# A hybrid decoder step: unbudgeted last top-ks, early key transpositions in the score products' PSUM tiles, and PLE weight splits on ScalarE and VectorE

## The chip, the cores and the metric

The kernel runs on one core of a Trainium2 chip. The metric is the device time of one execution in microseconds; the median of three runs before the change is 1889.77 us (1889.49 to 1900.7). The profile shows one further execution of the same program, with every engine's instructions: TensorE (PE), VectorE (DVE), ScalarE (ACT), GpSimd (POOL), and the queue of the sync engine (SP), which issues nearly all transfers.

## The reference

One layer over a prompt of 2048 rows and 64 sample rows. Cut to what bears on the change:

```python
z = rmsnorm(x, norm_g) @ w_in              # split into q, k, v, qi, ki, wi, ga, u, vm, gm
score = sum_h wi[h] * relu(qi[h] @ ki.T)   # indexer scores
idx = top_k(where(causal, score, -inf), 256)     # keys of each query row
o = softmax(q @ k[idx].T / 8) @ v[idx]           # per block of 128 rows
mix = concat(o * silu(ga), gelu(u) * s * silu(gm))
r = x + mix @ w_out
y = r + sigmoid(rmsnorm(r, ple_norm_g) @ w_ple_gate) * (p @ w_ple_proj)
```

Everything is fp32. A product is made from two fp32r parts of each factor, a high part and the remainder (hi and lo), in three matmuls: hi·hi, hi·lo and lo·hi.

## The kernel before

The prompt is cut into 16 blocks of 128 rows, and the sample rows are block 16, written SB in the code. There are three phases.

**Phase A** computes the input projection in rounds, and between its steps `pump` gives out pieces of the indexer: score products (PE writes them into the PSUM tiles `dots`, of which there are two), and top-ks (a search on ACT and DVE for the threshold of each row, ending in a mask that is written to `s_mask`). `pump` takes a budget of work and counts each piece against it. At the end of phase A stands the part of the output projection that needs no attention: for each block, `gm_load` reads the gated rows from `s_gm`, `gm_split` (L567) transposes them on PE into a PSUM tile `tp` (two buffers) from which ACT makes `hhi` (L124) and DVE the remainder (L125), and `gm_product` makes one output half as 12 matmuls into `z` (L579, L580, L583). I call these 12 matmuls a unit. ACT copies `z` out as `hlo` (L585) and SP writes it to `s_r` (L588). There are 34 units, two of them (block 16) with 8 matmuls.

The counter `u` numbers the units. From `u > EARLY` on, each unit lets the generator `early` go one step. At `u == DRAIN`, `pump(1e9)` gives out all that is left of the indexer and `early` becomes `prep_early`, which prepares the attention: it transposes the query blocks (L1036, two groups of four) and the 16 key tiles (L1021, four transposes each) into PSUM tiles that its argument supplies. For a key tile i, SP loads `b_kr` and `b_vr` (L991, L992; two buffers each), ACT doubles the keys into `b_kd` (L1015; two buffers), PE transposes, ACT writes `Kst` (L1023), DVE subtracts the remainder in it (L1024), and POOL makes the value parts `Vst` (L1026, L1027). At `u == FLAG_AT` a matmul of one column (L897) sums a flag of all top-ks, DVE writes it as `f_fl` (L899), and each engine reads it (L902) ahead of a branch that decides on a repeat of the search for rows where the threshold failed.

**Phase B** is the attention per block, scores `b_s` first (L1103, L1104). **Phase C** does the rest of the output projection (from `w_out`), the norm, and the last two products with `w_ple_gate` and `w_ple_proj`. These weights come as 8 and 2 tiles of 128 rows: `raw_load` (L1415) puts one into `c_raw` (three buffers) and `raw_split` makes `c_h` (L1421 on ACT, L1423 on another engine) and `c_l` (L1424). The residual row block is `c_x` (L1437, POOL), the norm's statistics are `c_st` (L1495, L1496, POOL), and the normed rows `c_rn` (L1497, DVE).

The program is not run in the order of the code: a scheduler orders each engine's queue at build time, and every engine then works its queue in order. An engine waits at an instruction until its operands are ready and the tile it writes is free.

Of the kernel before, what the change touches and what calls it, by code (L numbers as in the profile page):

```python
# [9 lines left out]
F32 = mybir.dt.float32  # L10
# [101 lines left out]
class Builder:  # L112
# [85 lines left out]
    def phase_a(self, eb):  # L198
        tc, nc, I, O = self.tc, self.nc, self.I, self.O
        with ExitStack() as es:  # L200
# [95 lines left out]
            def load_out(j):  # L296
                wh, wl = (t.rearrange("p k n -> p (k n)")[:, :2048].rearrange("p (k n) -> p k n", k=4) for t in halves(328))
                for i in range(8):
                    raw = rp.tile([128, 328], F32, name="raw")[:, :256]
                    k, c0 = i // 2, i % 2 * 256  # L300
                    nc.sync.dma_start(raw, I["w_out"][0, 512 + k * 128:640 + k * 128, j * 512 + c0:j * 512 + c0 + 256])
                    nc.gpsimd.tensor_scalar(wh[:, k, c0:c0 + 256], raw, 1.0, 1.0, op0=OP.mult, op1=OP.mult)
                    nc.gpsimd.tensor_tensor(wl[:, k, c0:c0 + 256], raw, wh[:, k, c0:c0 + 256].bitcast(F32), OP.subtract)
                return wh, wl
# [141 lines left out]
            blocks_due, dots, tops = [], [], []  # L446

            primed, active, steps = [], [None], [0]

            credit, turn = [0.0], [0]  # L450

            def pump(budget):
                credit[0] = min(credit[0], 0.0) + budget
                while credit[0] > 0 and (blocks_due or primed or dots or tops):
                    if not primed and blocks_due and not (dots and (active[0] == SB or steps[0] < 4)):
                        b = blocks_due.pop(0)
                        primed.append((b, self.sample_idx() if b == SB else self.idx(b)))
                        next(primed[0][1])
                    if not dots and primed and len(tops) < 2:
                        active[0], g = primed.pop()  # L460
                        steps[0] = 0
                        dots.append(g)
                    turn[0] ^= 1
                    l = (dots, tops)[turn[0]]
                    if l:
                        try:
                            v = next(l[0])
                            steps[0] += l is dots
                            if isinstance(v, tuple):
                                tops.append(self.topk(*v))  # L470
                                v = 0
                            credit[0] -= v
                            if l is tops and not (dots or primed or blocks_due):
                                tops.append(tops.pop(0))
                        except StopIteration:
                            l.pop(0)
# [15 lines left out]
            for si, (r, c) in enumerate(seq):  # L492
                blocks = ROUNDS[r]
                name = CH[c][0]
# [63 lines left out]
            def gm_load(b):  # L558
                gm[b] = hp.tile([128, 8, 128], F32R, name="hlo").rearrange("p a b -> p (a b)").bitcast(F32)[:self.rows(b)]
                nc.sync.dma_start(gm[b][:, :512], self.s_gm[b][:self.rows(b)])  # L560

            def gm_split(b):
                P = self.rows(b)
                hh = gmT[b] = hp.tile([128, 8, 128], F32R, name="hhi")
                ps = self.tp.tile([128, 4, 128], F32, name="tp")
                for k in range(4):
                    nc.tensor.transpose(ps[:, k, :P], gm[b][:, k * 128:k * 128 + 128], ident[:P, :P])  # L567
                if b == SB:
                    self.split(hh[:, 0:4, 0:64], hh[:, 0:4, 64:128], ps[:, :, 0:64])
                else:  # L570
                    self.split(hh[:, 0:4], hh[:, 4:8], ps)

            def gm_product(b, j, w):
                P = self.rows(b)
                hh = gmT[b]
                wh, wl = w
                zt = self.zp.tile([128, 512], F32, name="z")
                for k in range(4):
                    nc.tensor.matmul(zt, lhsT=hh[:, k], rhs=wh[:, k], start=(k == 0), stop=False)  # L579
                    nc.tensor.matmul(zt, lhsT=hh[:, k], rhs=wl[:, k], start=False, stop=(b == SB and k == 3))  # L580
                if b != SB:
                    for k in range(4):
                        nc.tensor.matmul(zt, lhsT=hh[:, 4 + k], rhs=wh[:, k], start=False, stop=(k == 3))  # L583
                y = gm[b][:, (1 - j) * 512:(1 - j) * 512 + 512]
                nc.scalar.activation(y, zt[:P], AF.Copy)  # L585
                if b == SB:
                    nc.vector.tensor_tensor(y, zt[64:128], y, OP.add)
                nc.sync.dma_start(self.s_r[b][:P, j * 512:j * 512 + 512], y)  # L588

            order = list(range(NB)) + [SB]  # L590
            early, u = iter(()), 0
            for n in range(0, 17, 2):
                if n == 0:
                    for b in order[:2]:
                        gm_load(b)
                    for b in order[:2]:
                        gm_split(b)
                for j in range(2):
                    for b in order[n:n + 2]:
                        gm_product(b, j, ws[j])  # L600
                        if n == 0 and j == 0 and b == 0:
                            ws.append(load_out(1))
                        if j == 1 and b + 2 < 17:
                            gm_load(b + 2)
                        pump(self.idx_rate)
                        u += 1
                        if u > EARLY:
                            next(early, None)
                        if u == DRAIN:
                            pump(1e9)  # L610
                            ei.close()
                            early = self.prep_early(eb, lambda: self.tp.tile([128, 4, 128], F32, name="tp"))
                        if u == FLAG_AT:
                            self.flag(self.tp.tile([128, 4, 128], F32, name="tp")[:, 0])
                for b in order[n + 2:n + 4]:
                    gm_split(b)
# [774 lines left out]
    def phase_c(self):  # L1391
        tc, nc, I, O = self.tc, self.nc, self.I, self.O
        V = nc.vector
        ident = self.ident
        with ExitStack() as es:
# [10 lines left out]
            tp = pool("c_tp", 2, space=PSUM)  # L1406
# [10 lines left out]
            def raw_split(name, k, eh, el):  # L1417
                hi, lo = W[name][k]
                raw = raw_tiles.pop((name, k))
                if eh is nc.scalar:  # L1420
                    nc.scalar.activation(hi, raw, AF.Copy)  # L1421
                else:
                    eh.tensor_scalar(hi, raw, 1.0, 1.0, op0=OP.mult, op1=OP.mult)  # L1423
                el.tensor_tensor(lo, raw, hi.bitcast(F32), OP.subtract)  # L1424
# [4 lines left out]
            def load(b):  # L1429
                P = self.rows(b)  # L1430
                mix = pre.tile([128, 512], F32, name="c_mix", bufs=2)[:P]
                r = pre.tile([128, D], F32, name="c_r")[:P]
                x = xp.tile([128, D], F32, name="c_x")[:P]
                nc.sync.dma_start(mix, self.s_o[b][:P])
                nc.sync.dma_start(r, self.s_r[b][:P])
                nc.sync.dma_start(x, I["x_sample"].rearrange("a t d -> (a t) d") if b == SB else I["x_prompt"][0, b * 128:b * 128 + 128])
                nc.gpsimd.tensor_tensor(x, x, r, OP.add)  # L1437
                st[b] = (mix, x)
# [45 lines left out]
            def stage1a(b):  # L1484
                mid[b] = transposed(b, st[b][0], 4, "o")
# [51 lines left out]
            gates = [("w_ple_gate", k) for k in range(8)] + [("w_ple_proj", k) for k in range(2)]  # L1537
# [3 lines left out]
            for n in range(LEAD + 1):  # L1541
                load(blocks[n + 1])
                stage1b(blocks[n])
                stage1a(blocks[n + 1])
                for q in range(n * per, min(n * per + per, len(gates))):
                    raw_split(*gates[q], nc.gpsimd if q % 3 == 2 else nc.scalar, nc.gpsimd if q % 3 == 1 else V)
                    if q + 3 < len(gates):
                        raw_load(*gates[q + 3])
            for n in range(2):
# [37 lines left out]
```

## Time and profile before

| | |
|---|---|
| Median of three runs | 1889.77 us |
| Profiled execution | 1893.5 us, of which the span is 1891.7 us |
| PE busy | 1833.5 us (97%) |
| DVE, ACT, POOL busy | 66%, 54%, 33% |
| Mean granted PE clock | 0.988 of full speed |

The span runs from the first to the last instruction of the profiled execution. Rows of the timeline give start, duration, engine, line, and the tile written with those read; in brackets stands the engine's idle time just before the row and what released it. A repeated matmul is one row with its count. A matmul's shown duration includes its pipeline; the spacing of starts tells its cost.

### The profile page before, as it was taken

The page shows a single profiled execution, that of the slowest core. Times are in us where ns is not written, and L with a number is a line of the kernel's source. Part 1 is how long each engine was busy: PE and PEld are TensorE (multiplying, and loading weights), DVE is VectorE, ACT ScalarE, POOL GpSimd, SP SyncE. Part 2 cuts the span into 40 slices and gives each one's busy share as a digit, 9 for nine tenths or more (in the row PEclk, how much of TensorE's full clock was granted, in tenths as well). Part 3 has the DMA queues.
Part 4 walks back from the last instruction along what each step waited for, and adds up shares of the span by engine and source line. Part 5 has one row for each costly group of instructions (what it writes and reads, how often), then busy time and mean ns, then how long its engine had stood idle before and what let it go on. Part 6 is the DMA issues. An engine that isn't in the chain of part 4 may idle for free.

```text
span 1891.7 us, 33962 instructions
## 1 busy us (share of the span) xinstructions
PE 1833.5 (97%) x11974; PEld 1601.0 (85%) x11974; DVE 1242.1 (66%) x3631; ACT 1018.2 (54%) x1909; POOL 623.5 (33%) x950
## 2 busy tenths in 40 slices
PE   7989998999999999999988899999999999999998
PEld 7989988999999999999877678778777777888887
DVE  5597665378878547788752789888999764233321
ACT  4244335256565636766654888868788653122121
POOL 5482562342012324013303442233221364222221
PEclk9989999999999999999999899999999999999999
DMA  8855756645344554554553442233220373223211
GB/s 253 247 163 179 223 189 203 215 131 161 119 162 146 194 174 145 163 170 134 176 188 128 134 112 76 64 108 94 61 78 12 100 258 122 74 95 104 94 37 45
DMA packets 243806, 261.53 MB, mean 138 GB/s; under 512 B 83176, under 2 KB 209840, under 8 KB 243248
## 3 DMA queue, kind: packets, MB, share of 16 engines
q1 hardware_dynamic: 237744, 240.45, 40.5%
q0 software_dynamic: 5888, 18.88, 3.4%
q8 instruction: 95, 1.56, 0.3%
q14 instruction: 79, 0.65, 0.1%
HBM read 171.90 MB, written 87.37 MB: 137 GB/s over the span
## 4 chain that ended last, share of the span: by engine, by line
PE 83%; DVE 5%; DMA 5%; POOL 2%; issue 2%; ACT 2%; SPq 0%; DVEq 0%; POOLq 0%; ACTq 0%
PE z L319 10%; PE z L320 10%; PE z L322 10%; PE b_o L1155 7%; PE b_tp L1138 6%; PE c_mm L1471 5%; PE c_mm L1470 5%; PE c_mm L1474 5%; PE b_s L1103 3%; PE dots L688 3%; PE dots L689 3%; PE b_s L1104 3%; PE z L579 1%; PE z L580 1%; PE z L583 1%
## 5 line engine op out<-in xcount | busy, mean ns | idle before, releaser
L319 PE MATMUL z<-whi,hhi 128*128 128x256 f32 (+1 forms) x1792 | 463.0, 292 | 10.5 <-ACT vt L414 5.0
L320 PE MATMUL z<-wlo,hhi 128*128 128x256 f32 (+1 forms) x1792 | 454.1, 287 | 0.2 <-DVE wlo L289 0.2
L319 PEld LDWEIGHTS z<-whi,hhi 128*128 128x128 f32 x1792 | 341.9, 191 | 21.2 <-issue 8.5
L320 PEld LDWEIGHTS z<-wlo,hhi 128*128 128x128 f32 x1792 | 341.8, 191 | 6.1 <-DVE wlo L289 1.5
L322 PE MATMUL z<-whi,hlo 128*128 128x256 f32 (+1 forms) x1792 | 262.6, 286 | 0.0
L322 PEld LDWEIGHTS z<-whi,hlo 128*128 128x128 f32 x1792 | 237.7, 190 | 2.0
L693 DVE SCALAR_TENSOR_TENSOR big<-dots,sgn,big 128x1024 f32<-128x1024 f32 (+7 forms) x176 | 179.2, 1018 | 52.3 <-ACT dots L691 50.6
L125 DVE TENSOR_TENSOR b_pt<-b_tp,b_pt 128x512 fp32r<-128x512 f32 (+1 forms) x288 | 183.4, 655 | 12.1 <-ACT b_pt L124 11.0
L691 ACT ACTIVATE dots<-dots 128x1024 f32<-128x1024 f32 (+7 forms) x176 | 140.3, 801 | 87.7 <-PE dots L689 82.9
L1155 PE MATMUL b_o<-b_pt,Vst 128*128 128x512 f32 x544 | 184.1, 424 | 1.2 <-DVE b_pt L125 0.8
L124 ACT ACTIVATE b_pt<-b_tp 128x512 fp32r<-128x512 f32 (+1 forms) x288 | 155.5, 578 | 48.2 <-PE b_tp L1138 45.4
L1138 PE MATMUL b_tp<-mats,b_sm 128*128 128x128 f32 x1088 | 172.0, 275 | 2.3 <-DVE b_pt L125 1.8
L1112 ACT ACTIVATE b_sm<-b_sm,b_st 128x128 f32<-128x128 f32 (+15 forms) x128 | 154.7, 1210 | 16.2 <-DVE b_st L1105 15.4
L829 ACT ACTIVATE bfw<-big,tk 128x384 bf16<-128x384 f32 (+14 forms) x105 | 136.4, 1300 | 45.7 <-DVE tk L849 27.9
L1138 PEld LDWEIGHTS b_tp<-mats,b_sm 128*128 128x128 f32 x1088 | 131.5, 141 | 34.1 <-ACT b_sm L1112 4.8
L1103 PE MATMUL b_s<-Kst,b_qh 128*128 128x512 f32 (+3 forms) x320 | 139.5, 439 | 4.1 <-DVE b_st L1105 2.2
L1105 DVE CUSTOM_DVE_ANT_0 b_sm<-b_s,b_mask,b_st 128x512 f32<-128x512 f32 (+3 forms) x192 | 123.9, 646 | 22.6 <-PE b_s L1104 17.8
L1104 PE MATMUL b_s<-Kst,b_ql 128*128 128x512 f32 (+3 forms) x320 | 117.6, 370 | 0.0
L688 PE MATMUL dots<-ki_stack,qih 128*128 128x512 f32 (+3 forms) x304 | 113.0, 373 | 3.1 <-DVE mk L833 3.1
L689 PE MATMUL dots<-ki_stack,qil 128*128 128x512 f32 (+3 forms) x304 | 110.2, 371 | 0.0
L1471 PE MATMUL c_mm<-c_l_w_ple_gate,c_mh 128*128 128x512 f32 x272 | 106.7, 392 | 3.2 <-DVE c_l_w_ple_gate L1424 2.1
L1470 PE MATMUL c_mm<-c_h_w_ple_gate,c_mh 128*128 128x512 f32 x272 | 109.0, 401 | 0.0
(351 smaller groups left out, 3747.0 us busy)
## 6 DMA issues: line engine op xcount, KB each, us to landing
whi<-s_wh SPq DMA_DIRECT2D x52, 512.0 KB
wlo<-s_wl SPq DMA_DIRECT2D x52, 512.0 KB
raw<-w_in SPq DMA_DIRECT2D x112, 128.0 KB
s_wh<-whi SPq DMA_DIRECT2D x13, 1024.0 KB
s_wl<-wlo SPq DMA_DIRECT2D x13, 1024.0 KB
b_qr<-s_q SPq DMA_DIRECT2D x32, 256.0 KB
s_r<-hlo SPq DMA_DIRECT2D x32, 256.0 KB
c_r<-s_r SPq DMA_DIRECT2D x16, 512.0 KB
```

The lines of the kernel that those rows point to most:

```text
L125: nc.vector.tensor_tensor(lo, src, hi.bitcast(F32), OP.subtract)
L319: nc.tensor.matmul(z, lhsT=hh[:, k], rhs=wh[:, k, :n], start=(k == 0), stop=False)
L320: nc.tensor.matmul(z, lhsT=hh[:, k], rhs=wl[:, k, :n], start=False, stop=False)
L322: nc.tensor.matmul(z, lhsT=hl[:, k], rhs=wh[:, k, :n], start=False, stop=(k == 7))
L688: nc.tensor.matmul(ps[:, s0:s0 + sn], lhsT=qh[h // 4][:, h % 4], rhs=rhs, start=True, stop=False)
L693: nc.vector.scalar_tensor_tensor(a, r, self.sgn[:, b, h:h + 1], a, op0=OP.mult, op1=OP.add)
L1103: nc.tensor.matmul(ps, lhsT=qh[:, h], rhs=rhs, start=True, stop=False)
L1104: nc.tensor.matmul(ps, lhsT=ql[:, h], rhs=rhs, start=False, stop=True)
L1138: nc.tensor.transpose(ps[:, k, r], sm2[r][:, (k0 + k) * 128:(k0 + k) * 128 + 128], ident)
L1155: nc.tensor.matmul(o.rearrange("p a b -> p (a b)"), lhsT=Vst[:, kb, g].rearrange("p a d -> p (a d)"), rhs=pt[:, k].rearrange("p a b -> p ( ...
L1470: nc.tensor.matmul(z, lhsT=hi[:, k], rhs=wts[k][0][:, ns], start=(k == 0), stop=False)
L1471: nc.tensor.matmul(z, lhsT=hi[:, k], rhs=wts[k][1][:, ns], start=False, stop=(b == SB and k == nk - 1))
```

## The change

Three edits. In `pump`, pieces are counted against the budget only while score products remain; when only top-ks are left, their steps cost nothing, so they are all given out by the next call. After DRAIN, the early query and key transposes get the two `dots` PSUM tiles (each cut to its first 512 columns) instead of the two `tp` tiles, which `gm_split` uses too. In phase C every high part of the ten PLE weight tiles is made by ACT and every remainder by DVE; before, POOL made three of the high parts (q = 2, 5, 8) and three of the remainders (q = 1, 4, 7).

```diff
@@ pump
-                            credit[0] -= v
+                            if dots or primed or blocks_due:
+                                credit[0] -= v
@@ after DRAIN
-                            early = self.prep_early(eb, lambda: self.tp.tile([128, 4, 128], F32, name="tp"))
+                            early = self.prep_early(eb, lambda: self.dp.tile([128, 1024], F32, name="dots")[:, :512]
+                                                    .rearrange("p (a b) -> p a b", a=4))
@@ phase C
-                    raw_split(*gates[q], nc.gpsimd if q % 3 == 2 else nc.scalar, nc.gpsimd if q % 3 == 1 else V)
+                    raw_split(*gates[q], nc.scalar, V)
```

Lines behind the first edit stand one further down in the changed kernel, those behind the second two further (L1021 becomes L1023).

On every engine the order is the same in both kernels up to the units behind DRAIN. PE before the change, at the third key tile: L1021 is the key transpose, L567 the transposes of `gm_split` for blocks 10 and 11, and the rest are matmuls of units.

```order
5018 L579 MATMUL z<-whi,hhi 128x512
5019 L580 MATMUL z<-wlo,hhi 128x512
5020 L583 MATMUL z<-whi,hhi 128x512 x4
5021 L1021 MATMUL tp<-mats,b_kd 128x128 x4
5022 L567 MATMUL tp<-mats,hlo 128x128 x8
5023 L579 MATMUL z<-whi,hhi 128x512
5024 L580 MATMUL z<-wlo,hhi 128x512
```

PE in the changed kernel, first where the transposes of block 10 now stand (L568), six units earlier than before, and then where the third key tile stands (L1023, two tiles at once), four units later than before and behind the flag (L899).

```order
5003 L581 MATMUL z<-wlo,hhi 128x512
5004 L584 MATMUL z<-whi,hhi 128x512 x4
5005 L568 MATMUL tp<-mats,hlo 128x128 x4
5006 L580 MATMUL z<-whi,hhi 128x512
5007 L581 MATMUL z<-wlo,hhi 128x512
```

```order
5061 L581 MATMUL z<-wlo,hhi 128x512
5062 L584 MATMUL z<-whi,hhi 128x512 x4
5063 L899 MATMUL tp<-f_sm 1x1
5064 L1023 MATMUL dots<-mats,b_kd 128x128 x8
5065 L580 MATMUL z<-whi,hhi 128x512
5066 L581 MATMUL z<-wlo,hhi 128x512
```

The key transposes no longer share a ring of tiles with `gm_split`, and the third to sixteenth stand two at a time among the last ten units.

SP before the change, at the read of the flag (L902): all loads of keys (L991) and values (L992) stand ahead of it.

```order
508 L991 DMA b_kr<-k_prompt 128x256
509 L588 DMA s_r_170<-hlo 128x512
510 L991 DMA b_kr<-k_prompt 128x256
511 L588 DMA s_r_171<-hlo 128x512
512 L991 DMA b_kr<-k_prompt 128x256
513 L902 TENSOR_LOAD f_fl
514 L902 ISA x2
515 L588 DMA s_r_172<-hlo 128x512
```

SP in the changed kernel at the same read (L904): L993 loads keys, L994 values.

```order
497 L993 DMA b_kr<-k_prompt 128x256
498 L904 TENSOR_LOAD f_fl
499 L904 ISA x2
500 L994 DMA b_vr<-v_prompt 128x256
501 L589 DMA s_r_169<-hlo 128x512
502 L994 DMA b_vr<-v_prompt 128x256 x2
503 L589 DMA s_r_170<-hlo 128x512
504 L994 DMA b_vr<-v_prompt 128x256
505 L993 DMA b_kr<-k_prompt 128x256 x2
506 L994 DMA b_vr<-v_prompt 128x256
```

Eight key loads (tiles 8 to 15) and nine value loads (7 to 15) now stand behind the read of the flag, and the loads of key tiles 8 and 9 behind those of the values 7 to 10.

POOL in phase C before the change: L1437 is the residual sum of a block, L1423 and L1424 the weights' parts, L1495 and L1496 the statistics of the norm.

```order
748 L1437 TENSOR_TENSOR c_x<-c_x,c_r 128x1024
749 L1424 TENSOR_TENSOR c_l_w_ple_gate<-c_raw,c_h_w_ple_gate 128x1024
750 L1495 TENSOR_SCALAR c_st<-c_st 128x1
751 L1496 TENSOR_TENSOR c_st<-c_st,c_mh 128x1
752 L1495 TENSOR_SCALAR c_st<-c_st 128x1
753 L1496 TENSOR_TENSOR c_st<-c_st,c_mh 128x1
754 L1437 TENSOR_TENSOR c_x<-c_x,c_r 128x1024
755 L1424 TENSOR_TENSOR c_l_w_ple_gate<-c_raw,c_h_w_ple_gate 128x1024
756 L1423 TENSOR_SCALAR c_h_w_ple_gate<-c_raw 128x1024
757 L1437 TENSOR_TENSOR c_x<-c_x,c_r 128x1024
```

POOL at the same place in the changed kernel (L1439, L1497, L1498): no part of the PLE weights is left on it.

```order
752 L1439 TENSOR_TENSOR c_x<-c_x,c_r 128x1024
753 L1497 TENSOR_SCALAR c_st<-c_st 128x1
754 L1498 TENSOR_TENSOR c_st<-c_st,c_mh 128x1
755 L1439 TENSOR_TENSOR c_x<-c_x,c_r 128x1024
756 L1497 TENSOR_SCALAR c_st<-c_st 128x1
```

DVE in phase C of the changed kernel, from the fourth to the ninth remainder (L1426), with the normed rows (L1499) among them; L125 is a remainder of transposed activations and L1494 a sum out of PSUM.

```order
3564 L1426 TENSOR_TENSOR c_l_w_ple_gate<-c_raw,c_h_w_ple_gate 128x1024
3565 L1499 SCALAR_TENSOR_TENSOR c_rn<-c_x,c_st,c_gb 128x1024
3566 L1426 TENSOR_TENSOR c_l_w_ple_gate<-c_raw,c_h_w_ple_gate 128x1024
3567 L1494 TENSOR_TENSOR c_x<-c_mm,c_x 128x1024
3568 L1426 TENSOR_TENSOR c_l_w_ple_gate<-c_raw,c_h_w_ple_gate 128x1024
3569 L125 TENSOR_TENSOR c_ml<-c_tp,c_mh 128x512 x2
3570 L1426 TENSOR_TENSOR c_l_w_ple_gate<-c_raw,c_h_w_ple_gate 128x1024
3571 L1499 SCALAR_TENSOR_TENSOR c_rn<-c_x,c_st,c_gb 128x1024
3572 L1426 TENSOR_TENSOR c_l_w_ple_gate<-c_raw,c_h_w_ple_gate 128x1024
3573 L1494 TENSOR_TENSOR c_x<-c_mm,c_x 128x1024
3574 L1426 TENSOR_TENSOR c_l_w_ple_proj<-c_raw,c_h_w_ple_proj 128x1024
3575 L125 TENSOR_TENSOR c_pl<-c_tp,c_ph 128x256
```

The remainders of all ten tiles are now DVE's, in the row in which it also makes the normed rows.

## Rows read from the trace of the kernel before

**Rows 1.** The page's first part: busy time, share of the span, instructions.
```profile
PE 1833.5 (97%) x11974; PEld 1601.0 (85%) x11974; DVE 1242.1 (66%) x3631; ACT 1018.2 (54%) x1909; POOL 623.5 (33%) x950
```

**Rows 2.** Windows behind DRAIN: length, busy of PE, PEld, DVE, ACT, POOL; clock, DMA.
```profile
981.00:991.00 10.00, 3.66 (x14) 3.15 (x15) 7.41 (x26) 3.33 (x7) 2.15 (x4) 0.68 0.37 122
...
1001.00:1011.00 10.00, 6.84 (x30) 5.33 (x29) 2.68 (x4) 3.37 (x7) 5.67 (x10) 0.87 0.63 200
...
1021.00:1031.00 10.00, 8.97 (x48) 7.07 (x48) 2.92 (x5) 4.29 (x8) 0.00 (x0) 1.00 0.27 96
1031.00:1041.00 10.00, 8.92 (x50) 7.27 (x49) 2.90 (x5) 5.16 (x10) 0.00 (x0) 1.00 0.22 81
```

**Rows 3.** Timeline of PE: the unit after DRAIN, and the first attention scores.
```profile
950.01 1.07 PE L583 MATMUL z<-whi,hhi 128*128 128x512 f32 x4
950.92 0.39 PE L579 MATMUL z<-whi,hhi 128*128 128x512 f32 x1
...
1045.07 0.33 PE L1103 MATMUL b_s<-Kst,b_qh 128*128 128x128 f32 x1 [1.41 <-DVE hlo L587]
```

**Rows 4.** Timeline of PE at the third key tile.
```profile
976.79 1.07 PE L583 MATMUL z<-whi,hhi 128*128 128x512 f32 x4
...
979.51 1.07 PE L583 MATMUL z<-whi,hhi 128*128 128x512 f32 x4
986.78 1.12 PE L1021 MATMUL tp<-mats,b_kd 128*128 128x128 f32 x4 [6.20 <-DVE Kst L1024]
```

**Rows 5.** Timeline of DVE at the same time.
```profile
980.60 1.76 DVE L865 MAX8 v<-big 128x8 f32<-128x1536 f32 x1
...
986.03 1.30 DVE L1024 TENSOR_TENSOR Kst<-tp,Kst 64x512 fp32r<-64x512 f32 x2
```

**Rows 6.** Timeline of PE, 1003 to 1013 us.
```profile
1003.05 0.60 PE L1021 MATMUL tp<-mats,b_kd 128*128 128x128 f32 x4
1003.49 0.60 PE L567 MATMUL tp<-mats,hlo 128*128 128x128 f32 x4
...
1007.91 0.50 PE L579 MATMUL z<-whi,hhi 128*128 128x512 f32 x1 [1.31 <-ACT hhi L124]
...
1012.36 0.60 PE L1021 MATMUL tp<-mats,b_kd 128*128 128x128 f32 x4
```

**Rows 7.** Timeline of SP's queue: a key load is issued.
```profile
1000.42 0.42 SPq L991 DMA_DIRECT2D b_kr<-k_prompt  x1
```

**Rows 8.** Timeline of ACT: the same key tile doubled, and the next.
```profile
1003.55 0.62 ACT L1015 COPY b_kd<-b_kr 128x512 f32<-128x512 f32 x1 [2.39 <-DMA b_kr<-k_prompt]
...
1006.74 0.62 ACT L1015 COPY b_kd<-b_kr 128x512 f32<-128x512 f32 x1 [1.58 <-DMA b_kr<-k_prompt]
```

**Rows 9.** Timeline of POOL: the first value tiles, and the ninth.
```profile
988.22 0.77 POOL L1026 TENSOR_SCALAR Vst<-b_vr 128x256 fp32r<-128x256 f32 x2 [36.78 <-DMA s_mask<-bfw]
...
1001.77 0.41 POOL L1026 TENSOR_SCALAR Vst<-b_vr 128x256 fp32r<-128x256 f32 x1 [0.84 <-DMA b_vr<-v_prompt]
```

**Rows 10.** Timeline of PE: the two longest waits of phase C.
```profile
1563.13 0.50 PE L1471 MATMUL c_mm<-c_l_w_ple_gate,c_mh 128*128 128x512 f32 x1 [2.09 <-DVE c_l_w_ple_gate L1424]
1566.14 0.50 PE L1471 MATMUL c_mm<-c_l_w_ple_gate,c_mh 128*128 128x512 f32 x1 [1.16 <-POOL c_l_w_ple_gate L1424]
```

**Rows 11.** Timeline of POOL in phase C.
```profile
1557.62 2.03 POOL L1423 TENSOR_SCALAR c_h_w_ple_gate<-c_raw 128x1024 fp32r<-128x1024 f32 x1
1559.62 2.36 POOL L1437 TENSOR_TENSOR c_x<-c_x,c_r 128x1024 f32<-128x1024 f32 x1
```

**Rows 12.** Timeline of DVE in phase C: a remainder undisturbed, and one beside POOL.
```profile
1540.46 1.22 DVE L1424 TENSOR_TENSOR c_l_w_ple_gate<-c_raw,c_h_w_ple_gate 128x1024 fp32r<-128x1024 f32 x1
...
1559.69 3.38 DVE L1424 TENSOR_TENSOR c_l_w_ple_gate<-c_raw,c_h_w_ple_gate 128x1024 fp32r<-128x1024 f32 x1 [0.94 <-POOL c_h_w_ple_gate L1423]
```

**Rows 13.** Groups by line, 1525 to 1575 us: busy us, mean ns, idle before.
```profile
L1421 ACT ACTIVATE c_h_w_ple_gate<-c_raw 128x1024 fp32r<-128x1024 f32 x6 | 6.2, 1056 | 7.9 <-DMA c_raw<-w_ple_gate 7.9
```

**Rows 14.** Window of phase C, columns as in rows 2.
```profile
1555.00:1565.00 10.00, 7.90 (x38) 5.76 (x36) 9.06 (x7) 4.00 (x6) 9.83 (x6) 1.00 0.56 169
```

## Prediction, before the result was seen

> **What bounds the kernel now.** The page's first part comes first: PE is busy for 1833.5 of 1891.7 us [rows 1], so a change to other engines pays only where PE waits or runs slowly. I then cut the trace into windows and looked for stretches near the three edits in which PE is not full. There are two.
>
> The first is the tail of the output projection behind DRAIN. It runs from the end of the first unit there, whose last group starts at 950.01 and ends at 951.08, to the first attention score at 1045.07 [rows 3], 93.99 us. In windows of 10 us PE is idle for 6.34, 3.16, 1.03 and 1.08 us [rows 2]; with the 1.41 us before the first score [rows 3] that is 13.0 us. In two of these windows the granted clock is 0.68 and 0.87 of full speed [rows 2].
>
> The largest hole, 6.20 us before 986.78, is at the third key tile, and the row names DVE's remainder of an earlier key tile as the releaser [rows 4]. On DVE that remainder starts at 986.03 only because it stands in the queue behind the last top-k, whose 1.76 us operation runs at 980.60 [rows 5]. PE cannot step over the transpose, so the transposes of blocks 10 and 11 and all units behind wait too. The reason is the shared ring: the two `tp` tiles are held by key tiles 0 and 1. Later holes repeat this at a smaller size: key load, doubling, transposition, Kst, and only then a free `tp` tile for the next `gm_split` (the 1.31 us wait before 1007.91 [rows 6]).
>
> The second stretch is phase C's start: 2.09 us before 1563.13 (remainder made by DVE) and 1.16 us before 1566.14 (remainder made by POOL) [rows 10], 3.25 us in all.
>
> **Edit 1, the budget.** Up to DRAIN the queues hold the same instructions in the same order, and at DRAIN the unlimited budget gave everything out before too. I cost it at nothing. What hides it is that the top-k already ends at about the same time: if DVE's new order delays the end, it delays the key remainders and the value tiles (below), not PE.
>
> **Edit 2, the tiles.** How many matmuls must PE run from 951.08 to the first score? 22 units of 12, two of 8, 25 groups of four transposes (16 keys, 2 queries, 7 `gm_split`), and one of 64 rows. A unit takes 979.51 − 976.79 = 2.72 us at full clock [rows 4]; two of 8 matmuls are 16/12 of that, 3.63. Four transposes take 1003.49 − 1003.05 = 0.44 us [rows 6]. The sum is 59.84 + 3.63 + 11.0 + about 0.25 = 74.7 us. So of 93.99 us, 19.3 are not work at full speed: 13.0 idle, the other 6.3 a slow clock. The slow clock is visible: the unit at 1007.91 takes 4.45 us to the next transpose at 1012.36, where 2.72 is normal [rows 4, 6].
>
> In the changed order nothing waits for DVE's top-k until the flag: block 10's transposes stand six units earlier and need only `tp`, and only key tiles 0 and 1 are transposed before the flag. I replayed that order with the durations of the rows. PE then has 14 units and 11 groups of transposes without a hole up to the flag: 951.08 + 14 × 2.72 + 11 × 0.44 = 994.0. The top-k ends near 985.6 (some 1.5 us later than before, as DVE's remainders of `gm_split` stand among its steps), so the flag does not wait. DVE's key remainders start then, 8 us before PE asks for a `dots` tile.
>
> Behind the flag the key tiles come in pairs, and each must be loaded and doubled. A load that SP issues at 1000.42 [rows 7] lets ACT start the copy at 1003.55 [rows 8]: 3.13 us, plus 0.62 for the copy. Key tile 8's load stands behind the loads of values 7 to 10, and the load of value 10 needs value 8 finished. Before, the first value tile started at 988.22 and the ninth (value 8) at 1001.77 [rows 9]. With the mask some 1.8 us later, value 8 starts at 1003.6 and ends about 1.15 later; its successor's load and then the key's are issued by about 1005.5, and the doubled key is ready by 1005.5 + 3.13 + 0.62 = 1009.2. PE asks for it at about 1011.0. The margin is 1.8 us there and about 1 us for tile 9, and over 3 us for the last six. The replay puts the first score at 1026.9 (951.08 + 74.7 is 1025.8, and 1.1 of the wait before it stays), a gain of 18.2 us. Its bounds: 19.3 at best, and nothing if each pair waits as in the first rival. I take off half a load chain, 1.6 us, because two margins are thinner than what the replay is good for, and round to **16.5 us**. Behind the branch phase B has its old order and PE is its bound, so I let it shift as a whole.
>
> **Edit 3, the weights.** It takes three high parts (2.03 us, the one in rows 11) and three remainders off POOL and puts three high parts of 1.06 us on ACT [rows 13], which sits idle for 7.9 us waiting for loads in this stretch [rows 13], and three remainders of 1.22 us [rows 12], 3.66 us, on DVE. That DVE shows 9.06 of 10 us busy [rows 14] speaks against the edit, but part of that is stretch: the remainder at 1559.69 takes 3.38 us and not 1.22 [rows 12], beside POOL's 2.36 us sum that began at 1559.62 and ends at 1561.98 [rows 11]. The remainder ends 1.09 us after that, so it all but ran when POOL was done. POOL has less work after the change but keeps these sums. Both waits of PE are for late remainders, and the raw tiles come free earlier, so their loads start earlier. Bounds: 3.25 us gained, or 3 us lost if DVE takes POOL's place (third rival). Nearest is the undisturbed 1.22 us row: **3.0 us**.
>
> The Trainium skill, "SBUF — State Buffer", section "SBUF: two separate sides", says that a VectorE operation with two SBUF inputs and a GpSimd operation that reads SBUF lock each other out for a whole instruction. The trace agrees, with 3.38 us beside 1.22. By that rule each of the ten remainders on DVE can meet one of POOL's sums, and the edit's gain could turn into the third rival's loss; by the rows' undisturbed price the sum stays at 3.0.
>
> **Sum.** 16.5 + 3.0 = 19.5 us. From the profiled execution's own 1893.5 that is 1874.0. This execution was 3.7 us above the median; from the median the forecast is 1889.8 − 19.5 = **1870.3 us**.
>
> **Rivals.**
> 1. *The key tail waits for loads.* The order speaks for it: eight key loads and nine value loads now stand behind the flag's read in SP's queue, and only two buffers of each exist, so a load can't run far ahead. If each of the six last pairs waits one chain (3.13 + 0.62) less the unit beside it (2.72), that is 1.0 us each, 6 us, and three units at the slow clock cost 3 × (4.45 − 2.72) = 5.2 more. The gain falls to 8.3: 1881.5. Against it: the replayed margins. Chance 0.17.
> 2. *The time is given back in phase B.* The first scores come early, but queries, masks or value tiles for the first blocks arrive at their old time. Then edit 2 keeps perhaps a fifth, 3 us: 1887, or 1884 with edit 3. Against it: the values are prepared from about 990, some 35 us before the first score. Chance 0.10.
> 3. *DVE takes POOL's place in phase C.* If all three new remainders meet a POOL sum, each takes 3.38 us in place of 1.22; DVE's queue grows by 10.1 us where its window has 0.94 us idle [rows 14], and I let PE wait for the eighth gate tile 3 us longer than now. Edit 3 then loses 3 instead of gaining 3: 1876.3, inside the range.
> 4. *Slower.* SP's queue is the place. Suppose the eight key loads behind the flag run one at a time, each behind a value load that waits too. PE reaches key tile 8 at about 1011 less the margins, say 1001 with nothing to do in between; the kernel loses over 1% when the first score falls behind 1045 + 19 + 3 (what edit 3 gives) = 1067, that is from (1067 − 1001)/8 = 8.3 us per key on. Two chains in a row are 7.5, and the unit beside them at the slow clock adds 1.7: 9.2 us, first score at 1074.6, 29.5 us late, 1889.8 + 29.5 − 3.0 = 1916. Against it: the rows show a key load landing 3.2 us behind the last one's copy [rows 8], with values running beside. Chance 0.05.
>
> **How the numbers follow.** The likeliest case, 0.68, has its own range from 1867.2 (all 22.55 us recovered) to 1876.3 (rival 3). The range of 8 in 10 takes in rival 1: 1867 to 1884; outside are rivals 2 and 4, 0.15, and a little below. A measurement of this kernel can tell about 1% from no change, 18.9 us, so faster begins below 1870.9; my forecast is just below that line. About 0.62 of the likeliest case lies below it: 0.42 faster. The rest of it and rivals 1 and 2 are within 1%: 0.53. Slower: 0.05.
>
> **What would show it.** In the profile after: no wait over 1 us on PE between 951 and 994; the flag near 994; the first score near 1027; the clock 1.00 in these windows; eighth and later key transposes preceded by idle time that names ACT's `b_kd` or a `b_kr` load (rival 1). In phase C no wait of PE for `c_l`; if one is left with DVE as releaser and remainders of 2 to 3.4 us, it is rival 3. The start of phase C's first `w_out` matmuls should come as much earlier as the first score did; if less, rival 2. The prediction is wrong in its main term if the first score falls after 1032.

## The result, and the profile after

The changed kernel takes 0.9923 times what the kernel before takes, with a 95% interval of 0.9907 to 0.9939. The medians of the runs side by side are 1878.95 us (8 runs, 1875.3 to 1881.41) and 1892.2 us (8 runs). Of 1892.2 us the ratio is 14.6 us, with 11.5 to 17.6 for the interval. I had forecast 19.5 us, on the median of the three runs shown 1870.3 us, with a range of 1867 to 1884. The measured time is in the range, but the 19.5 us lie above the interval of the gain. Of the two terms of the sum, one came as forecast and the other came with the wrong sign.

The profiled execution after took 1876.23 us, with a span of 1874.2 us. To see where the time went I compare the start of the same instruction in both traces. PE starts the first unit of the output projection at 914.80 before and 911.46 after. These 3.3 us lie ahead of the change, where the order is the same, and they are the difference of two executions (in the other runs this start lies between 912.38 and 915.66). From there on, with the line numbers of the kernel before:

| stretch | before | after | difference |
|---|---|---|---|
| first unit of the output projection to the first attention score | 130.26 | 113.58 | −16.68 |
| to the 61st `b_o` matmul of L1155 (head of phase B) | 76.15 | 74.82 | −1.33 |
| to the first matmul with `w_out` (rest of phase B) | 411.74 | 412.02 | +0.28 |
| to the 151st matmul of L1470 (start of phase C) | 116.49 | 119.88 | +3.39 |
| to the last matmul of L1474 | 235.04 | 235.04 | 0.00 |

The sum is −14.3 us, close to what the ratio gives.

The windows after, with the columns of [rows 2], show the first gain. PE is full from 951 to 1021 us, at full clock, where before it stood idle and slow.

```profile
981.00:991.00 10.00, 10.00 (x49) 8.10 (x47) 5.83 (x23) 3.75 (x7) 2.58 (x5) 1.00 0.50 173
...
1001.00:1011.00 10.00, 10.00 (x54) 8.11 (x53) 2.51 (x4) 4.68 (x9) 6.30 (x12) 1.00 0.53 170
```

The timeline of PE after has the flag, the third and fourth key tile (L1023) without any wait, and the first score, which answers to [rows 3, 4].

```profile
991.15 0.19 PE L899 MATMUL tp<-f_sm 128*1 128x1 f32 x2
991.27 1.09 PE L1023 MATMUL dots<-mats,b_kd 128*128 128x128 f32 x8
...
1025.03 0.33 PE L1105 MATMUL b_s<-Kst,b_qh 128*128 128x128 f32 x1 [0.51 <-DVE hlo L588]
```

The wait of 6.20 us at the third key tile is gone. On DVE the key remainders still stand behind the last top-k (L1026 first starts at 986.71), but PE no longer needs them before 991.

In phase C the two waits of [rows 10] have another shape. The timeline of PE after:

```profile
1545.25 0.79 PE L1472 MATMUL c_mm<-c_h_w_ple_proj,c_ph 128*128 128x512 f32 x1 [2.37 <-ACT c_ph L124]
1546.59 0.80 PE L1473 MATMUL c_mm<-c_l_w_ple_gate,c_mh 128*128 128x512 f32 x1 [0.54 <-DVE c_l_w_ple_gate L1426]
1547.18 3.62 PE L1476 MATMUL c_mm<-c_h_w_ple_gate,c_ml 128*128 128x512 f32 x8
```

One matmul of `w_ple_proj` now stands among those of the gate, waits 2.37 us for ACT's `c_ph`, and behind the wait PE is slow: eight matmuls take 3.4 us to the next start at 1550.59, where they take 1.84 before. The window from 1543 to 1553 has PE busy for 7.21 of 10 us at a clock of 0.66; the trace's clock record has half speed (1.2 GHz) from 1544.26 to 1551.09, and before the change none in this phase. The idle time of PE is much the same as before: 2.37 and 0.54 with two waits ahead of them of 0.16 and 0.48 make 3.55 us, against 3.25. What the kernel loses here is the slow clock: PE works for 5.30 of its 6.83 us, which by the eight matmuls (3.41 us against 1.84) costs about 2.4 us.

ACT's timeline after shows why `c_ph` is late, and SP's the loads.

```profile
1519.49 1.06 ACT L1496 ACTIVATE c_rn<-c_x 128x1024 f32<-128x1024 f32 x1 [4.46 <-DVE c_mh L1528]
...
1520.55 2.95 ACT L1423 ACTIVATE c_h_w_ple_gate<-c_raw 128x1024 fp32r<-128x1024 f32 x3
...
1543.87 1.06 ACT L1423 ACTIVATE c_h_w_ple_proj<-c_raw 128x1024 fp32r<-128x1024 f32 x1 [3.09 <-DMA c_raw<-w_ple_proj]
1544.84 0.36 ACT L124 ACTIVATE c_ph<-c_tp 128x256 fp32r<-128x256 f32 x1
```

```profile
1525.07 0.33 SPq L1417 DMA_DIRECT2D c_raw<-w_ple_gate  x1
...
1539.80 2.66 SPq L1417 DMA_DIRECT2D c_raw<-w_ple_proj  x2
```

`c_ph` takes 0.36 us, but it stands in ACT's queue behind a high part of `w_ple_proj`, and ACT waits 3.09 us for that load. The chain begins much earlier. ACT makes the first three high parts at 1520.55, behind the first block's square sum (L1496), for which it waits 4.46 us. That is 8.7 us behind the first `w_out` matmul (1511.87). Before the change ACT made its first two high parts at 1536.01, ahead of the square sum, 3.1 us behind the first `w_out` matmul (1532.95). So the raw tiles come free later: the first reload is issued 13.2 us behind the first `w_out` matmul, and before it was 8.8.

Only half of these 4.4 us is the order. The timelines of POOL and DVE have the other half, and why the last gate remainder is late.

```profile
1521.55 2.40 POOL L1439 TENSOR_TENSOR c_x<-c_x,c_r 128x1024 f32<-128x1024 f32 x1
1521.63 5.68 DVE L1426 TENSOR_TENSOR c_l_w_ple_gate<-c_raw,c_h_w_ple_gate 128x1024 fp32r<-128x1024 f32 x3 [2.16 <-ACT c_h_w_ple_gate L1423]
...
1542.02 3.38 DVE L1499 SCALAR_TENSOR_TENSOR c_rn<-c_x,c_st,c_gb 128x1024 f32<-128x1024 f32 x1
1545.32 1.21 DVE L1426 TENSOR_TENSOR c_l_w_ple_gate<-c_raw,c_h_w_ple_gate 128x1024 fp32r<-128x1024 f32 x1
```

The first of the three remainders takes 3.41 us beside POOL's sum, where 1.22 is undisturbed. It ends at 1525.04, and the reload of its tile is issued at 1525.07. In e5, the same program, the second remainder meets the sum (3.40 us), and the second reload is the one that is held up. The last gate remainder, whose high part is done at 1540.78, stands behind a normed row of 3.38 us (1.27 undisturbed, at 1527.84), also beside a sum of POOL. PE takes it up at 1546.59, so without the wait for `c_ph` it would have waited for this remainder.

### The profile page after: what moved, and what is told of

It is laid out like the page before. It is cut to its first block, busy times and chain, and to the rows that moved or that the text cites. A ratio compares the mean times of both kernels' runs of the same rounds, so it can differ in the third digit from the quotient of the medians.

```text
span 1874.2 us, 33958 instructions
## 1 busy us (share of the span) xinstructions
PE 1829.9 (98%) x11974; PEld 1597.5 (85%) x11974; DVE 1243.5 (66%) x3634; ACT 1020.5 (54%) x1912; POOL 609.6 (33%) x944
## 5 line engine op out<-in xcount | busy, mean ns | idle before, releaser
L125 DVE TENSOR_TENSOR b_pt<-b_tp,b_pt 128x512 fp32r<-128x512 f32 (+1 forms) x288 | 183.1, 654 | 11.8 <-ACT b_pt L124 11.0
L1157 PEld LDWEIGHTS b_o<-b_pt,Vst 128*128 128x128 f32 x544 | 89.4, 189 | 22.7 <-DVE b_pt L125 7.5
```

Source lines behind the costliest of these rows:

```text
L125: nc.vector.tensor_tensor(lo, src, hi.bitcast(F32), OP.subtract)
L1157: nc.tensor.matmul(o.rearrange("p a b -> p (a b)"), lhsT=Vst[:, kb, g].rearrange("p a d -> p (a d)"), rhs=pt[:, k].rearrange("p a b -> p ( ...
```

## The experiments

The table has the ratio to the kernel before, and from each profile the two stretches that the change touches: the first unit to the first score (stretch A), and the first `w_out` matmul to the 151st matmul of L1470 (start of C).

| kernel | ratio (95%) | stretch A | start of C |
|---|---|---|---|
| before | 1 | 130.26 | 116.49 |
| the change | 0.9923 (0.9907 to 0.9939) | 113.58 | 119.88 |
| e5, the change again | 0.9936 (0.9925 to 0.9948) | 113.34 | 120.32 |
| e1, without edit 3 | 0.9906 (0.9892 to 0.9920) | 114.26 | 117.03 |
| e12, the same again | 0.9920 (0.9903 to 0.9936) | 113.49 | 118.50 |
| e4, keys only, without edit 3 | 0.9909 (0.9893 to 0.9925) | 113.68 | 114.54 |
| e3, queries only, without edit 3 | 1.0007 (0.9995 to 1.0018) | 130.91 | 115.93 |
| e2, edit 3 alone | 0.9991 (0.9978 to 1.0004) | 130.21 | 113.14 |
| e6, one `w_ple_proj` high part on POOL | 0.9948 (0.9936 to 0.9960) | 113.90 | 122.08 |
| e7, only the remainders moved | 0.9932 (0.9919 to 0.9945) | 113.80 | 121.85 |
| e8, `w_ple_proj` loaded first | 0.9931 (0.9918 to 0.9944) | 113.29 | 120.10 |
| e9, the change, first high parts early | 0.9926 (0.9909 to 0.9943) | 114.47 | 116.57 |
| e10, edit 3 alone, first high parts late | 1.0006 (0.9995 to 1.0017) | 129.12 | 118.80 |
| e11, without edit 3, first high parts early | 0.9911 (0.9890 to 0.9932) | 113.24 | 114.37 |

The stretches are those of one profiled execution each. Kernels with the same order in phase C, row for row, differ there by 0.56 us (before and e3) and by 2.5 us (e1 and e4).

Edit 1 needed no run of its own. With edit 1 alone every engine's queue, as it is built, is that of the kernel before, row for row, but for the numbers of some tiles; and edit 2 with it and without it are the same too.

**Which edit gave the gain?**

```diff
# e1: edits 1 and 2; phase C as before
-  raw_split(*gates[q], nc.scalar, V)
+  raw_split(*gates[q], nc.gpsimd if q % 3 == 2 else nc.scalar, nc.gpsimd if q % 3 == 1 else V)
# e2: edit 3 only, on the kernel before
-  raw_split(*gates[q], nc.gpsimd if q % 3 == 2 else nc.scalar, nc.gpsimd if q % 3 == 1 else V)
+  raw_split(*gates[q], nc.scalar, V)
```

> Edits 1 and 2 only; the PLE weights are split as before. Theory: edit 2 gave all of the gain (16.7 us up to the first score, 1.3 us in the head of phase B) and edit 3 took 3.4 us back, so this kernel is 18.0 us faster than before (ratio 0.9905) and about 3.4 us faster than the full change; in phase C the two waits of 2.09 and 1.16 us are back and the clock stays at 1.00. Rival: edit 3 is neutral or gains, and the loss seen in phase C comes from phase B's earlier start: then 14.6 us faster or less, with PE waiting for c_ph here too.

> Edit 3 only. Theory: PE waits about 2 us or more behind ACT's first high part of w_ple_proj, the clock falls after it, and the kernel is 3 us slower than before (ratio 1.0016, 1.000 to 1.003). Rival (the forecast): DVE's remainders come in time and it is 3.0 us faster (0.9984).

e1 came at 0.9906, as expected: edit 2 carries the whole gain. In phase C it is not quite as expected: there is one wait, of 2.65 us for a gate remainder, and behind it 3.41 us at half speed. e2 was a miss for my theory of that moment. Edit 3 alone is not 3 us slower; its profile has phase C's start at 113.14 us, 3.35 us shorter than before, with no wait of PE for a weight left. That is what I had forecast for edit 3. In time it is 0.9991, with 1 inside the interval, so the gain is seen in the trace and not in the runs. In the traces, then, edit 3 shortens the phase by itself, and lengthens it beside edit 2. ACT's and SP's timeline of e2 show the difference to the full change:

```profile
1537.14 2.95 ACT L1421 ACTIVATE c_h_w_ple_gate<-c_raw 128x1024 fp32r<-128x1024 f32 x3
1541.70 1.06 ACT L1494 ACTIVATE c_rn<-c_x 128x1024 f32<-128x1024 f32 x1 [1.61 <-DVE c_mh L1526]
```

```profile
1542.84 1.46 SPq L1415 DMA_DIRECT2D c_raw<-w_ple_gate  x2
```

Here the high parts come ahead of the square sum, 3.1 us behind the first `w_out` matmul (1534.08), and the first reloads 8.8 us behind it.

**Which transposes did the sharing hurt?**

```diff
# e3: edits 1 and 2 for the queries only
-  prep_kv(i, psum)
+  prep_kv(i, lambda: self.tp.tile([128, 4, 128], F32, name="tp"))
# e4: edits 1 and 2 for the keys only
-  prep_q(ORDER[0], psum)
+  prep_q(ORDER[0], lambda: self.tp.tile([128, 4, 128], F32, name="tp"))
```

> Edit 1, and edit 2 for the query transposes only: the key transposes stay in the tp ring. Theory: the ring shared by keys and gm_split is the cause, so the hole of about 6 us before the third key tile stays and the time is that of before, 0 to 3 us faster. Rival: the queries' place is what counts, 10 us faster or more.

> Edit 1, and edit 2 for the key transposes only: the two groups of query transposes stay in the tp ring. Theory: as edits 1 and 2 together, 18 us faster (0.9905). Rival: the queries held the ring, 10 us faster or less.

Both as the theory had it. With the keys left in the `tp` ring the hole stays, 6.00 us:

```profile
984.10 1.12 PE L1021 MATMUL tp<-mats,b_kd 128*128 128x128 f32 x4 [6.00 <-DVE Kst L1024]
```

With only the keys moved, the time is 0.9909 and no wait stands on PE between 951 and 1020. So the place of the key transposes in the ring that `gm_split` uses is shown as the cause. That the tiles were held until DVE had worked off the top-k is read from [rows 4, 5]. The tiles and the order that the scheduler makes with them changed together, and no run parts the two.

**What does edit 3 cost beside edit 2?** First I blamed the matmul of `w_ple_proj` that stands early in PE's order.

```diff
# e6: the full change, but
-  raw_split(*gates[q], nc.scalar, V)
+  raw_split(*gates[q], nc.gpsimd if q == 8 else nc.scalar, V)
# e7: edits 1 and 2, and
+  raw_split(*gates[q], nc.gpsimd if q % 3 == 2 else nc.scalar, V)
# e8: the full change, but
-  gates = [("w_ple_gate", k) for k in range(8)] + [("w_ple_proj", k) for k in range(2)]
+  gates = [("w_ple_proj", k) for k in range(2)] + [("w_ple_gate", k) for k in range(8)]
```

> The full change once more, beside the variants of edit 3. Theory: the loss in phase C is built into this order of PE (one matmul of w_ple_proj stands after 15 of the first block's 32 matmuls with c_mh and waits for ACT's first high part of w_ple_proj), so it shows again: a wait of 1 us or more for c_ph, a slow clock behind it, and 14 to 15 us faster than before (0.9923). Rival: it was this one execution's loads; then phase C gains here as edit 3 alone did in its profile, and the kernel is 20 us faster (0.989).

> The full change, except that the high part of the first w_ple_proj tile stays on GpSimd, as before the change. In PE's order no matmul of w_ple_proj stands among the gate's any more. Theory: no wait for c_ph, phase C 3 us shorter than before the change, 21 us faster in all (0.989). Rival: DVE's ten remainders or ACT's load are the cause whatever the order; then it is as the full change, 14.6 us faster (0.9923).

> Edits 1 and 2, and of edit 3 only the remainders on DVE (high parts as before). PE's order has no early matmul of w_ple_proj. Theory: phase C gains up to 3 us over the order before, 18 to 21 us faster in all (0.989 to 0.9905). Rival (DVE takes POOL's place, whatever the order): 15 us faster, with PE waiting for remainders.

> The full change, with the two w_ple_proj tiles loaded and split ahead of the eight w_ple_gate tiles. PE's order has matmuls of w_ple_proj early again (four behind 11 of the gate's), but their weights are there first. Theory: no wait for c_ph; the last two gate tiles come two places later, so PE may wait up to 3 us for a remainder of those: 16 to 21 us faster (0.989 to 0.9915). Rival: an early matmul of w_ple_proj costs as before, 14.6 us faster or less.

The loss is no accident of one execution: e5 repeats it, 120.32 us in phase C's start. But e6, which has no early matmul of `w_ple_proj`, gained nothing. It is the slowest of the group, and PE waits 4.54 us for the last gate remainder instead. e7, which moves no high part, does the same. It gained 12.9 us where the theory had 18 to 21; its rival, "DVE takes POOL's place", had 15 and PE waiting for remainders. The rows are from PE, POOL and DVE of e7:

```profile
1553.11 0.80 PE L1471 MATMUL c_mm<-c_l_w_ple_gate,c_mh 128*128 128x512 f32 x1 [5.05 <-DVE c_l_w_ple_gate L1424]
```

```profile
1547.65 2.34 POOL L1437 TENSOR_TENSOR c_x<-c_x,c_r 128x1024 f32<-128x1024 f32 x1
```

```profile
1547.72 3.36 DVE L1497 SCALAR_TENSOR_TENSOR c_rn<-c_x,c_st,c_gb 128x1024 f32<-128x1024 f32 x1 [0.44 <-POOL c_st L1496]
1551.00 2.05 DVE L1424 TENSOR_TENSOR c_l_w_ple_gate<-c_raw,c_h_w_ple_gate 128x1024 fp32r<-128x1024 f32 x1
```

ACT has the high part of that tile done at 1547.25, but on DVE the remainder stands behind a normed row that is stretched beside POOL's sum.

e8 removes the late load of `w_ple_proj` and is a miss too (13.1 us gained, 16 to 21 expected). The same wait is there with another load in its place: ACT now waits for a gate tile ahead of `c_ph`, and PE 2.53 us for `c_ph`.

```profile
1545.83 1.06 ACT L1421 ACTIVATE c_h_w_ple_gate<-c_raw 128x1024 fp32r<-128x1024 f32 x1 [3.26 <-DMA c_raw<-w_ple_gate]
```

So the early matmul is not the cause; whichever weight comes last is late. All these kernels have in common that ACT's high parts stand behind the square sum, and that DVE makes all ten remainders. Two experiments set that order by hand, with the weights' engines unchanged, and two stand beside them.

```diff
# e9: the full change, the first three tiles split ahead of the loop, and the square sum pinned behind them
+  for q in range(3):
+      step(q)                      # raw_split and the next raw_load
...
-  nc.scalar.activation(rn, x, AF.Square, accum_out=sq[:, 0:1])
+  a = nc.scalar.activation(rn, x, AF.Square, accum_out=sq[:, 0:1])
+  if b == blocks[0]:
+      tc.keep_in_program_order(a)
# e10: edit 3 alone, the first three tiles split behind stage1b of block 0, and pinned there
+  h = nc.scalar.activation(hi, raw, AF.Copy)
+  if name == "w_ple_gate" and k < 3:
+      tc.keep_in_program_order(h)
# e11: as e9, with the weights split over three engines as before; e12: e1 once more
```

> The full change, with one order pinned: ACT makes the first three high parts of w_ple_gate ahead of the first block's square sum (L1494), as it did before the change and with edit 3 alone. Theory (the loss is that order: high parts 5.6 us later, so the three raw tiles come free late and every later load with them): reloads at about 8.8 us behind the first w_out matmul, no wait over 1 us for c_ph or a gate remainder, phase C as short as with edit 3 alone (113 us between the first and the 151st hi matmul of phase C, against 120), 21 us faster than before (0.989). Rival (VectorE and GpSimd block each other more when DVE makes all remainders): 120 us, 14 us faster (0.9925).

> Edit 3 alone, with the opposite order pinned: the first three high parts of w_ple_gate behind ACT's square sum. Theory: the loss shows without edit 2: phase C 119 to 121 us instead of 113, a wait of 2 us or more with a slow clock behind it, 4 us slower than before (1.002). Rival: edit 2's earlier start of phase C is needed for the loss; then as edit 3 alone, 0.9984 to 0.9991.

> Edits 1 and 2, weights split as before over three engines, and the first high parts ahead of the square sum. Theory: phase C 114 to 117 us as before; 17 to 19 us faster (0.990 to 0.991), 2 to 4 us slower than e9_full_high_first. Rival (the order does not matter): the same as e9_full_high_first and as edits 1 and 2.

> Edits 1 and 2 once more, beside the pinned ones on the same chip. 18 us faster than before (0.9905); 3 us slower than e9_full_high_first by the theory, 4 us faster by its rival.

Put together, the runs give phase C's start by two things: where ACT's first high parts stand, and who makes the remainders.

| | remainders on DVE and POOL | all ten on DVE |
|---|---|---|
| high parts ahead of the square sum | before 116.49, e3 115.93, e11 114.37 | e2 113.14, e9 116.57 |
| high parts behind it | e1 117.03, e4 114.54, e12 118.50 | the change 119.88, e5 120.32, e6 122.08, e7 121.85, e8 120.10, e10 118.80 |

In e6 and e12 about 1.5 us are not of the weights: there the clock falls to half speed for 3.41 us at the first `w_out` matmul, and the square sum starts 9.1 us behind it and not 7.6. Without them e12 is as long as e1, and only the last cell is long. The late order alone costs nothing that can be told (e1, e4, e12), and neither do ten remainders on DVE alone (e2, e9). The loss needs both. The plainest pair is e1 and e7, whose code differs only in who makes three remainders: 4.8 us. The order is worth about 3.5 us beside edit 2 (e9 against the change and e5), not much more than the 2.5 us between e1 and e4, and 5.7 us without it (e10 against e2). Of those 5.7, 1.37 is a wait of PE for a remainder of the activations (`c_ol`), and not for a weight. Edit 2's earlier start of phase C is not needed for the loss, as e10 shows. What matters is the order that came with edit 2: the square sum stands first in every kernel with the keys moved that was not pinned.

The times bear this out in part only. e9 is a miss twice over. Its phase is not as short as e2's, and its ratio of 0.9926 is that of the full change and of its rival on record: what its profile gains in phase C is within what the executions of a kernel differ by. e11 and e12 were to come 2 to 4 us behind e9 and came ahead of it, and e10 was to be 4 us slower than before and came at 1.0006, with 1 inside the interval. The wait that is left in e9 is for the last gate remainder, and that remainder was stretched beside POOL's `c_x`, as in [rows 12]; the three rows are from PE, DVE and POOL.

```profile
1547.91 0.50 PE L1471 MATMUL c_mm<-c_l_w_ple_gate,c_mh 128*128 128x512 f32 x1 [2.26 <-DVE c_l_w_ple_gate L1424]
```

```profile
1544.47 3.38 DVE L1424 TENSOR_TENSOR c_l_w_ple_gate<-c_raw,c_h_w_ple_gate 128x1024 fp32r<-128x1024 f32 x1
```

```profile
1543.64 3.13 POOL L1437 TENSOR_TENSOR c_x<-c_x,c_r 128x1024 f32<-128x1024 f32 x1 [1.65 <-DMA c_r<-s_r]
```

POOL's sum ends at 1546.77 and the remainder at 1547.85, 1.08 us later. In e2 the same remainder began 28.0 us behind the first `w_out` matmul, took 1.23 us and nothing was lost. The stretch, 2.15 us, is nearly the whole wait of 2.26, so without it e9 would have lost little by this estimate.

The best that the runs support is the change without edit 3: e1, e4, e11 and e12 lie at 0.9906 to 0.9920. The full change and its kin with more remainders on DVE (e5 to e9) lie at 0.9923 to 0.9948. e1 and e12, the same program on two chips, differ by 0.0014, and their intervals overlap with that of the change, so an advantage for leaving edit 3 out is likely (about 3 us by the mean ratios of the four against the change and e5), but its size is not shown. Pinning the high parts first brings nothing that the runs can tell there (e11).

## Why the prediction was right, and where it was wrong

**What bounds the kernel.** Right: PE's holes and its slow clock behind DRAIN were what edit 2 could win, and it won them.

**Edit 1.** Right at nothing; the order of every engine shows it.

**Edit 2.** Forecast 16.5 us, measured 16.68 in stretch A. The path was as replayed. The flag comes 79.7 us behind the first unit, and the replay had 79.2 (994.0 − 914.8). The first score comes 113.58 us behind it, and the replay had 112.1 without its allowance. But the allowance of 1.6 us was spent on something else than I said, and that it had the right size is luck: no key tile waited for its load. Of the work that I summed, four transposes are a little dearer than 0.44: two key tiles with a unit between them start 3.22 us apart (954.40 and 957.62), where 2.72 + 0.44 makes 3.16; over 25 groups that is 1.5 us. The 6.3 us that I put down to the slow clock are too many for the same reason. The clock record of the kernel before has half speed for 10.24 us of this stretch, and PE works for 7.48 of them, so about 3.7 us were lost. PE's waits went from 13.44 us (I had 13.0) to 0.51. Together that is 16.7 us, which is what was gained. The margins I feared held: ACT ends doubling key tile 9 at 1007.58, and PE asks for it at 1009.36.

**The shift of phase B.** Nearly right. It gave 1.3 us more, for which I had no term. The stretch of slow clock at its head is 6.8 us long and before 10.2, but that does not explain it: e2 and e3, in the old order, have 6.8 us there too and need 75.88 and 76.01 us for the head, against 76.15 before. Kernels with the keys moved need 74.46 to 75.84. What shortens it stays open.

**Edit 3.** Wrong: forecast as a gain of 3.0 us, and 3.39 us lost in the trace. Two steps failed together. One is the price of a remainder, "Nearest is the undisturbed 1.22 us row". The other is "the raw tiles come free earlier". Both served for edit 3 alone (113.14 us, 3.35 gained). They fail beside edit 2, where ACT's order changes: high parts at 8.7 us and not 3.1, first reload at 13.2 and not 8.8, the first remainder and a normed row stretched to 3.41 and 3.38 us. The loss shows only where both things come together, ten remainders on DVE and the late high parts. I also took ACT's 7.9 us of idle time as room. It was ACT standing at the head of its queue for a load, with everything behind it held, and in the full change `c_ph` came late behind such a wait. But e7 moves no high part to ACT and is as long (121.85 us), so the loss does not hang on this step. The order of ACT and of PE in phase C was there to be read ahead of the result: I read POOL's and DVE's rows, and forecast from each edit by itself.

**The rivals.** Rival 1 (key loads), rival 2 (given back in phase B) and the slower case did not come. Rival 3 has the right place and the right size, −3 us, and half of the mechanism. I had DVE late because three new remainders meet POOL's sums at 3.38 us each. In the full change one gate remainder and one normed row show that stretch, and e7's and e9's last waits are of that kind. What I did not have is that it costs only beside the late high parts: e2's third remainder takes 3.42 us and nothing is lost. With rival 3 in place of the main case, its own number was 1876.3 by the old median: 13.5 us gained, and 14.6 measured. The likeliest case ended there, and the range went on to 1884 for rival 1, which did not come. So it is in part luck that the measured 1878.95 us lies inside; 2.4 us of it are the higher median of the kernel before.

By the Trainium skill, "SBUF — State Buffer", section "SBUF: two separate sides", a VectorE operation with two SBUF inputs and a GpSimd operation that reads SBUF lock each other out for a whole instruction. DVE's remainder and POOL's sum are such a pair, and e9's rows agree: the remainder ended 1.08 us after POOL's sum, though it had begun 2.30 us ahead of that end, and undisturbed it takes 1.22.

**The chances.** Faster by over 1% had 0.42 and did not come; within 1% had 0.53 and did.

## What to carry to other kernels

Two streams of work that take turns in a ring of PSUM tiles are tied together by their slowest reader: before tuning either, see who frees the tile and what stands ahead of that reader in its queue. An engine's idle time is room only where nothing that another engine needs stands behind the instruction that waits. And where a scheduler sets the order, an edit that shortens a phase by itself can lengthen it beside another: read the order of the combination on every engine that the second edit loads, at the place where it was meant to pay.

## What the runs showed of the hardware that was not expected

After the change the clock fell towards the end of a wait of 2.37 us, with two of 0.16 and 0.48 just ahead of it, and stayed at half speed for 6.83 us. Before the change waits of 2.09 and 1.16 us, 3 us apart, left the clock at full speed. The idle time is nearly the same, and the one phase is 3.4 us longer than the other. e9, with a single wait of 2.26 us, shows half speed for 3.41 us, e10 the same behind one of 2.10, and e11, with one of 1.52, none. So what a wait of about 2 us costs cannot be read from its length alone: in these traces it was the wait itself, or up to 3 us more.
